# Gate, up and K with weights still: 16 wide and 16 narrow products for two weight units instead of 4 and 4 for each k

## The chip, the core and the metric

The kernel runs on one core of a Trainium2 chip. The core has a matrix engine (TensorE, in the profile PE for the products and PEld for the loads of the stationary operand), VectorE (DVE), ScalarE (ACT), GpSimd (POOL) and a queue engine SyncE (SP) that issues transfers from HBM. The engines run on their own and meet at semaphores. The metric is the device time of one execution in microseconds (us): the median of three runs of the kernel before is 992.02 us.

## The reference

A trunk of two layers over 256 tokens with 1024 channels, in float32. Each layer has a SwiGLU FFN (2816 hidden channels), a token mixer and a second such FFN, with norms around them. The mixer of layer 0 is a recurrent block (RG-LRU), that of layer 1 an attention whose K, V and forget gates are computed once from the stream after layer 0. What the change touches are the gate, up and K products:

```python
def swiglu(x, w_gate, w_up, w_down):
    return (jax.nn.silu(x @ w_gate) * (x @ w_up)) @ w_down
...
hn = rms_norm(h, g)
kv = (hn @ w_kv).reshape(Bn, S, 2, N_HEADS, HEAD_DIM)
```

## The kernel before

**Split operands.** Each weight `w` is split into a high part `whi` (ScalarE, line 204: a copy with the rounding of fp32r) and a low part `wlo` (VectorE, line 205: what is left); so is the activation (`xhi`, `xlo`, side by side in `xall`). A product takes high x high, high x low and low x high.

**Weights still.** For most gate and up tiles and for K the weights are the stationary operand and the activations move. One call of `mmj` does one k, that is 128 of the 1024 input channels, for a tile of 512 output channels: four products with a 128x128 block of `whi` over 512 moving columns (`xhi` and `xlo` of all 256 tokens, line 238; I call them wide), each into a PSUM bank of its own, then four with a block of `wlo` over the 256 columns of `xhi` alone (line 240, narrow). The left and the right half of a bank are added up later (`total`, lines 511 and 512). Elsewhere (`mm3`, lines 212 to 214, in the down projections and others) the activation stands still and 512 columns of weights move; in the recurrent block (`mm3w`, lines 219 to 221) the weights stand still and 256 columns move.

**Units and tiles.** A weight unit is 128x1024 floats: two k of one tile. One transfer brings it into one of five `raw` buffers, and the split writes it into one of nine `whi` and nine `wlo` buffers. A tile takes four units (k0 = 0, 2, 4, 6). Gate tiles accumulate in banks 4 to 7, up tiles in banks 0 to 3, in turn; the two K tiles use banks 4 to 7, then 0 to 3. While a tile is at work its banks are `lent`. Behind a tile's last product stand `gate_rows`, `up_rows` or `post_k`, each beginning with `total`. The FFNs have 44, 36, 44 and 36 units of this kind and K has 8.

**Order.** TensorE runs its instructions in the order in which the program issues them; the other engines' orders are made by a scheduler. `run_ffn` calls `slot(None, i)` for each unit of the still part, clears `state["edge"]`, and goes on with the down projection. `slot` prepares the unit where that has not been done, calls its work, marks it in `done` and ticks. `still` does the two k of a unit with a tick between them. So a unit has two ticks.

**Ticks.** `tick` counts down the deferred work in `pend` and runs what is due, and it lets `prepare_next` issue the load and the split of one unit further on, if the estimated landing time has passed and the unit nine before is done. Work deferred with the flag `calm` is held back while `state["edge"]` is true. Before the change `edge` is true in the first and the last unit of a tile and false in the two between. The calm pieces are `gains_T` for the later gains (line 162), `rg_params` (line 710), `running(0)` and `running(1)` (running sums of the forget gates, lines 1065 and 1066) and `rows(0)` and `rows(1)` (line 1072, with the store of `ckT` behind it, which attention reads back). They take a free bank from `sparebank`: one of banks 0 to 3 that is neither held nor lent, otherwise 6 or 7.

**The start.** The first tile's work is interleaved by hand through `hooks`, keyed by k (1, 3 and 4): they transpose and split the activations and split the first five units.

Of the kernel before, what the change touches and what calls it, by code (L numbers as in the profile page):

```python
# [16 lines left out]
P = 128  # L17
D = 1024
S = 256
# [28 lines left out]
def trunk_kernel(ctx: ExitStack, tc: tile.TileContext, A: dict, out: bass.AP):  # L48
    nc = tc.nc
# [11 lines left out]
    def nm(s):  # L61
        uid[0] += 1
        return f"{s}_{uid[0]}"
# [33 lines left out]
    def sparebank():  # L97
        return bank("mm" if any(i not in held and i not in lent for i in range(4)) else "tr")
# [4 lines left out]
    def tensor_work(n):  # L103
        pace["t"] += n * 0.445e-3
# [5 lines left out]
    def defer(n, fn, calm=False):  # L110
        pend.append([n, fn, calm])

    def tick():
        for p in list(pend):
            p[0] -= 1
            if p[0] < 0 and not (p[2] and state["edge"]):
                pend.remove(p)
                p[1]()
        purse[0] = min(purse[0] + SHARE, SHARE)
        if state["p"] >= OPEN:  # L120
            prepare_next()
        while queue and purse[0] > 0:
            cost, _, fn = queue.pop(0)
            purse[0] -= cost
            fn()
# [98 lines left out]
    def x_moving(k):  # L224
        return xall[:, k, :, :], xhi[:, k, :]

    def mmj(bs, wh, wl, k, moving):

        both, upper = moving(k)
        o, oh = pall, pall[:, :, :S]  # L230
        if len(both.shape) == 4:
            o = o.rearrange("p n (a t b) -> p n a t b", a=2, t=2)
            oh = oh.rearrange("p n (t b) -> p n t b", t=2)
        else:
            o = o.rearrange("p n (a b) -> p n a b", a=2)
        tensor_work(3 * S * len(bs))
        for b, w in zip(bs, wh):
            nc.tensor.matmul(o[:, b], w, both, start=k == 0, stop=False)  # L238
        for b, w in zip(bs, wl):
            nc.tensor.matmul(oh[:, b], w, upper, start=False, stop=k == 7)  # L240


    def rstd_of(ss, n, f=1.0):
# [128 lines left out]
    items = []  # L372
    units = {}
    done = {}
    state = {"p": 0, "a": 0, "b": 0, "edge": False, "look": 99}
# [23 lines left out]
    def slot(t, i):  # L399
        while state["p"] <= i:  # L400
            prepare_next(True)
        items[i][1](t, units[i])
        done[i] = done.get(i, 0) + (1 if t is not None else 2)
        if done[i] == 2:
            units.pop(i)
        tick()
# [106 lines left out]

    hooks = {}

    def still(u, k0, b0, moving=x_moving):
        if k0 == 0:
            assert not set(held) & set(range(b0, b0 + 4)), held.keys()
            lent.update(range(b0, b0 + 4))
        state["edge"] = k0 in (0, 6)  # L520
        for j in range(2):
            if k0 + j in hooks:
                hooks.pop(k0 + j)()
            cut = [slice(j * 512 + b * P, j * 512 + b * P + P) for b in range(4)]
            mmj(range(b0, b0 + 4), [u.hi[:, c] for c in cut], [u.lo[:, c] for c in cut], k0 + j, moving)
            if j == 0:
                tick()
        if k0 == 6:
            lent.difference_update(range(b0, b0 + 4))
            state["edge"] = True  # L530

    def tile_items(w, c0, b0, post, moving=x_moving):
        for k0 in range(0, 8, 2):
            def prep(k0=k0):
                return split(load_raw(w[k0 * P:(k0 + 2) * P, c0:c0 + 512].rearrange("(k p) n -> p k n", p=P), P, 1024),
                             P, 1024)

            def work(t, u, k0=k0):
                still(u, k0, b0, moving)
                if k0 == 6:  # L540
                    post(b0, 4)
            items.append((prep, work))

    def ffn_items(pool_of, wg, wu, wd, post_g, next_dests, last=False, normed=False, lead=1):
        hid = {}
        sil = {}
        box = {}

        def hid_tiles():
            if not hid:  # L550
                v = hid["all"] = pool_of().tile([P, 2, 2, 22, P], F32R, tag="hid", name=nm("hid"), bufs=1)
                hid["hhi"], hid["hlo"] = v[:, 0], v[:, 1]
            return hid["hhi"], hid["hlo"]

        def gate_tile(n):
            return pool_of().tile([P, 1024], F32, tag="sil", name=nm("sil"), bufs=1)[:, :n]

        def prod_tile(n):
            return pool_of().tile([P, 16 * HA], F32, tag="prod", name=nm("prod"), bufs=1)[:, :n]

        def post_gate(t, ps):
            if t == 0:
                box["s"] = gate_tile(1024)
            s = sil[t] = box["s"][:, t * 512:(t + 1) * 512]
            nc.scalar.activation(s, ps, AF.Silu, scale=rs[t][:, 0:1])

        def post_up(c0):
            def f(t, ps):
                if t == 0:
                    box["p"] = prod_tile(1024)  # L570
                pr = box["p"][:, t * 512:(t + 1) * 512]
                nc.vector.tensor_tensor(pr, ps, sil[t], ALU.mult)
                defer(HT, lambda: hidden_T(pr, t))

            def hidden_T(pr, t):
                hh, hl = hid_tiles()
                tp = sparebank()
                for j in range(4):
                    nc.tensor.transpose(tp[:, j * P:(j + 1) * P], pr[:, j * P:(j + 1) * P], ident)
                k0 = c0 // P  # L580
                hv = hh[:, t, k0:k0 + 4, :].rearrange("p a b -> p (a b)")
                lv = hl[:, t, k0:k0 + 4, :].rearrange("p a b -> p (a b)")
                nc.scalar.activation(hv, tp, AF.Copy)
                nc.vector.tensor_tensor(lv, tp, hv.bitcast(F32), ALU.subtract)
            return f

        def gate_rows(b, m):
            s = sil["j"] = gate_tile(m * S)
            v = s.rearrange("p (a b) -> p a b", a=m)
            total(v, b, m)  # L590
            nc.vector.tensor_tensor(v, v, rcp["v"].unsqueeze(1).to_broadcast([P, m, S]), ALU.mult)  # L591
            nc.scalar.activation(s, s, AF.Silu)  # L592

        def up_rows(b, m, k0):
            pr = prod_tile(m * S)
            hh, hl = hid_tiles()
            total(pr.rearrange("p (a b) -> p a b", a=m), b, m)
            nc.vector.tensor_tensor(pr, pr, sil["j"], ALU.mult)  # L598
            pv = pr.rearrange("p (a t b) -> p a t b", a=m, t=2)
            hv = hh[:, :, k0:k0 + m, :].rearrange("p t a b -> p a t b")  # L600
            lv = hl[:, :, k0:k0 + m, :].rearrange("p t a b -> p a t b")
            nc.scalar.activation(hv, pv, AF.Copy)  # L602
            nc.vector.tensor_tensor(lv, pv, hv.bitcast(F32), ALU.subtract)

        def last_items(c0):
            for k0 in range(0, 8, 2):
                def prep(k0=k0):
                    raw = new_raw()
                    v = raw.rearrange("p (k s n) -> p k s n", k=2, s=2)
                    for s, w in enumerate((wg, wu)):  # L610
                        nc.sync.dma_start(v[:, :, s, :], w[k0 * P:(k0 + 2) * P, c0:c0 + 256].rearrange("(k p) n -> p k n", p=P))
                    return split(raw, P, 1024)

                def work(t, u, k0=k0):
                    still(u, k0, 4)
                    if k0 == 6:
                        gate_rows(4, 2)
                        up_rows(6, 2, c0 // P)
                items.append((prep, work))

        i0 = len(items)
        for i in range(5):
            if i < lead:
                proj_items(wg, i * 512, 512, main_x, post_gate)
                proj_items(wu, i * 512, 512, main_x, post_up(i * 512))
            else:
                tile_items(wg, i * 512, 4, gate_rows)
                tile_items(wu, i * 512, 0, lambda b, m, i=i: up_rows(b, m, 4 * i))
        last_items(2560)

        def load_gb():
            box["gb"] = gain_bcast(post_g)

        ahead(i0 + 24, load_gb)

        def post_down(t, accs):
            enter(t, next_dests(t, hid), accs, box["gb"], True, last, normed)

        i2 = len(items)
        row_items(wd, [P] * 22, lambda t, k: (hid["hhi"][:, t, k, :], hid["hlo"][:, t, k, :]), post_down, 4 if last else 2)  # L640
        return i0 + 8 * lead, i2, len(items)
# [472 lines left out]
    for n in range(2):  # L1114
        tile_items(A["w_kv"], n * 512, 4 - 4 * n, post_k(n), z_moving)
# [151 lines left out]
    for i in range(OPEN):  # L1267
        u = units[i] = Unit()
# [165 lines left out]
```

## Time and profile before

| what | value |
|---|---|
| median of three runs | 992.02 us (991.96 to 992.54) |
| the profiled execution, its own time | 992.25 us |
| its span, first to last instruction | 990.5 us |
| VectorE / ScalarE busy | 68% / 57% of the span |
| mean granted TensorE clock | 0.999 |
| read from HBM | 180.09 MB, 183 GB/s over the span |

The profile is one execution. Its times are counted from the span's start. In the timeline a row gives the start, the duration (merged over instructions of one kind that follow each other, with their number behind x), the engine, the line, the operation, the output and the inputs by name, the shapes, and in brackets idle time before it with what ended it. Products on PE are pipelined, their ends are modelled and they overlap: the distance between starts tells the rate, not the duration.

### The profile page before, as it was taken

What the parts mean: (1) busy time and instruction counts of PE and PEld (TensorE: products, weight loads), DVE (VectorE), ACT (ScalarE), POOL (GpSimd) and SP (SyncE); (2) the same over time, 40 slices, a digit from 0 to 9 for tenths busy, and PEclk for the clock granted to TensorE, in tenths of its full rate; (3) what the DMA queues carried; (4) which work ended last, traced back from release to release, by engine and by line L of the source; (5) the groups of instructions that cost most, each with busy time, mean ns of one, the idle gap of its engine ahead of it and who ended that gap; (6) DMA issues with size and microseconds to landing.
All of it is one profiled execution on the core that took longest, in us unless ns stands there. A gap on an engine that the chain in (4) does not pass through costs nothing.

```text
span 990.5 us, 13894 instructions
## 1 busy us (share of the span) xinstructions
PE 979.7 (99%) x5294; PEld 835.9 (84%) x5294; DVE 675.5 (68%) x791; ACT 563.3 (57%) x740; POOL 50.9 (5%) x97
## 2 busy tenths in 40 slices
PE   9999999999999999999999999999999999999997
PEld 7888888899978888888898888888887688888885
DVE  6877664668997776664696676674488867667542
ACT  6666543559986555543565555553467665555431
POOL 3300000100003000000000000000030000000000
PEclk9999999999999999999999999999999999999999
DMA  8777646565337766545468666654585157665431
GB/s 276 259 265 232 197 151 191 166 181 158 109 105 229 235 190 186 195 151 179 116 219 277 191 179 192 193 187 162 172 291 177 42 172 238 193 192 188 159 115 42
DMA packets 94088, 182.06 MB, mean 184 GB/s; under 512 B 11822, under 2 KB 33414, under 8 KB 93894
## 3 DMA queue, kind: packets, MB, share of 16 engines
q1 hardware_dynamic: 93350, 181.10, 58.3%
q8 instruction: 41, 0.67, 0.3%
q0 software_dynamic: 640, 0.07, 0.1%
q14 instruction: 25, 0.20, 0.1%
q10 hardware_dynamic: 32, 0.01, 0.0%
HBM read 180.09 MB, written 1.06 MB: 183 GB/s over the span
## 4 chain that ended last, share of the span: by engine, by line
PE 71%; issue 21%; ACT 3%; DVE 3%; POOL 1%; DMA 1%; SPq 0%; DVEq 0%; POOLq 0%; ACTq 0%
PE pall L238 24%; PE pall L240 12%; PE pall L212 9%; PE pall L214 9%; PE pall L213 9%; PE pall L856 1%; PE pall L219 1%; PE pall L220 1%; PE pall L221 1%; DVE wlo L205 1%; DMA raw<-in_ffn_w_gate_dram 1%; PE pall L1160 1%; POOL rstd L248 1%; ACT junk L253 1%; PE pall L1187 1%
## 5 line engine op out<-in xcount | busy, mean ns | idle before, releaser
L205 DVE TENSOR_TENSOR wlo<-raw,whi 128x1024 fp32r<-128x1024 f32 (+4 forms) x328 | 392.9, 1205 | 236.4 <-ACT whi L204 235.8
L204 ACT ACTIVATE whi<-raw 128x1024 fp32r<-128x1024 f32 (+4 forms) x328 | 340.1, 1044 | 284.2 <-PE pall L214 112.7
L238 PE MATMUL pall<-xall,whi 128*128 128x512 f32 x1280 | 348.7, 394 | 0.2 <-DVE xall L1284 0.2
L238 PEld LDWEIGHTS pall<-xall,whi 128*128 128x128 f32 x1280 | 219.0, 188 | 28.8 <-DVE xall L1284 0.7
L240 PEld LDWEIGHTS pall<-xall,wlo 128*128 128x128 f32 x1280 | 195.9, 188 | 28.0
L240 PE MATMUL pall<-xall,wlo 128*128 128x256 f32 x1280 | 203.7, 281 | 0.0
L212 PE MATMUL pall<-whi,hid 128*128 128x512 f32 (+2 forms) x400 | 153.0, 382 | 0.0
L214 PE MATMUL pall<-whi,hid 128*128 128x512 f32 (+2 forms) x400 | 152.5, 381 | 0.3 <-DVE hid L276 0.3
L213 PE MATMUL pall<-wlo,hid 128*128 128x512 f32 (+2 forms) x400 | 152.4, 381 | 0.0
L214 PEld LDWEIGHTS pall<-whi,hid 128*128 128x128 f32 x400 | 75.1, 188 | 14.4 <-DVE hid L276 0.6
L212 PEld LDWEIGHTS pall<-whi,hid 128*128 128x128 f32 x400 | 75.1, 188 | 13.6
L213 PEld LDWEIGHTS pall<-wlo,hid 128*128 128x128 f32 x400 | 75.1, 188 | 13.6
L246 POOL TENSOR_SCALAR nv<-ss 128x1 f32<-128x1 f32 x24 | 10.5, 438 | 925.5 <-ACT junk L253 925.4
L212 PE MATMUL pall<-whi,xall 128*128 128x512 f32 (+2 forms) x144 | 57.3, 398 | 0.0
L214 PE MATMUL pall<-whi,xall 128*128 128x512 f32 (+2 forms) x144 | 55.2, 384 | 0.0
L213 PE MATMUL pall<-wlo,xall 128*128 128x512 f32 (+2 forms) x144 | 55.0, 382 | 0.0
L592 ACT ACTIVATE sil<-sil 128x1024 f32<-128x1024 f32 (+1 forms) x22 | 21.7, 984 | 25.3 <-DVE sil L591 25.3
L602 ACT ACTIVATE hid<-prod 128x1024 fp32r<-128x1024 f32 (+1 forms) x22 | 21.6, 984 | 20.0 <-DVE prod L598 20.0
L214 PEld LDWEIGHTS pall<-whi,xall 128*128 128x128 f32 x144 | 27.0, 188 | 5.4 <-DVE xall L276 0.3
L212 PEld LDWEIGHTS pall<-whi,xall 128*128 128x128 f32 x144 | 27.1, 188 | 4.9
L213 PEld LDWEIGHTS pall<-wlo,xall 128*128 128x128 f32 x144 | 27.1, 189 | 4.5
L316 DVE SCALAR_TENSOR_TENSOR t<-pall,rstd,gb 128x512 f32<-128x512 f32 x16 | 11.8, 747 | 26.7 <-ACT junk L253 26.7
(193 smaller groups left out, 982.0 us busy)
## 6 DMA issues: line engine op xcount, KB each, us to landing
raw<-in_ffn_w_down_dram SPq DMA_DIRECT2D x88, 512.0 KB
raw<-in_ffn_w_up_dram SPq DMA_DIRECT2D x80, 512.0 KB
raw<-in_ffn_w_gate_dram SPq DMA_DIRECT2D x78, 512.0 KB
raw<-in_rg_w_in_dram SPq DMA_DIRECT2D x20, 504.0 KB
raw<-in_ffn_w_gate_dram SPq DMA_DIRECT2D x20, 256.0 KB
raw<-in_rg_w_out_dram SPq DMA_DIRECT2D x10, 504.0 KB
raw<-in_ffn_w_up_dram SPq DMA_DIRECT2D x16, 256.0 KB
raw<-in_w_kv_dram SPq DMA_DIRECT2D x8, 512.0 KB
```

The source lines that it names most:

```text
L204: nc.scalar.activation(hi[:parts, c:c + m], rawv[:, c:c + m], AF.Copy)
L205: nc.vector.tensor_tensor(lo[:parts, c:c + m], rawv[:, c:c + m], hi[:parts, c:c + m].bitcast(F32), ALU.subtract)
L212: nc.tensor.matmul(ps, xh, wh, start=first, stop=False)
L213: nc.tensor.matmul(ps, xh, wl, start=False, stop=False)
L214: nc.tensor.matmul(ps, xl, wh, start=False, stop=last)
L219: nc.tensor.matmul(ps, wh, xh, start=first, stop=False)
L238: nc.tensor.matmul(o[:, b], w, both, start=k == 0, stop=False)
L240: nc.tensor.matmul(oh[:, b], w, upper, start=False, stop=k == 7)
L246: nc.gpsimd.tensor_scalar(v, ss[:, 0:1], ss[:, 1:2] if n == 2 else 0.0, D * EPS * f * f, ALU.add, ALU.add)
L316: nc.vector.scalar_tensor_tensor(t1[n], pf[n], r_in, gb[:, n * 512:(n + 1) * 512], ALU.mult, ALU.mult)
L592: nc.scalar.activation(s, s, AF.Silu)
L602: nc.scalar.activation(hv, pv, AF.Copy)
```

## The change

`mmj` takes a list of k instead of one k, and does the wide products of all of them before the narrow ones. `still` takes a list of units. `grouped` puts the first unit of a pair by (k0 = 0 or 4, if no hooks are left); `slot` then ticks and returns without marking it done. With the second unit the pair is done at once: 16 wide products, 16 narrow ones, then three ticks, what stands behind the tile (`post`), and the tick of `slot`. `edge` is true where the group holds the first or the last k of a tile, so in both pairs of each tile. While hooks are left, units are done one at a time and one k at a time.

```diff
-    def mmj(bs, wh, wl, k, moving):
+    def mmj(bs, parts, ks, moving):
...
+        for k, (wh, wl) in zip(ks, parts):
+            tensor_work(2 * S * len(bs))
+            for b, w in zip(bs, wh):
+                nc.tensor.matmul(o[:, b], w, moving(k)[0], start=k == 0, stop=False)
+        for k, (wh, wl) in zip(ks, parts):
+            tensor_work(S * len(bs))
+            for b, w in zip(bs, wl):
+                nc.tensor.matmul(oh[:, b], w, moving(k)[1], start=False, stop=k == 7)
...
     def slot(t, i):
         while state["p"] <= i:
             prepare_next(True)
-        items[i][1](t, units[i])
+        if items[i][1](t, units[i]):
+            tick()
+            return
...
-    def still(u, k0, b0, moving=x_moving):
+    def still(us, k0, b0, moving=x_moving):
         if k0 == 0:
             assert not set(held) & set(range(b0, b0 + 4)), held.keys()
             lent.update(range(b0, b0 + 4))
-        state["edge"] = k0 in (0, 6)
-        for j in range(2):
+        n = 2 * len(us)
+        state["edge"] = k0 == 0 or k0 + n == 8
+        parts = []
+        for u in us:
+            for j in range(2):
+                cut = [slice(j * 512 + b * P, j * 512 + b * P + P) for b in range(4)]
+                parts.append(([u.hi[:, c] for c in cut], [u.lo[:, c] for c in cut]))
+        run_ = 1 if hooks else n
+        for j in range(0, n, run_):
             if k0 + j in hooks:
                 hooks.pop(k0 + j)()
...
+            mmj(range(b0, b0 + 4), parts[j:j + run_], range(k0 + j, k0 + j + run_), moving)
+            for _ in range(run_ if j + run_ < n else run_ - 1):
                 tick()
-        if k0 == 6:
+        if k0 + n == 8:
             lent.difference_update(range(b0, b0 + 4))
             state["edge"] = True
...
+    def grouped(k0, kept, fn):
+
+        i = len(items)
+
+        def work(t, u):
+            kept.append((i, u))
+            if len(kept) < 2 and not hooks and k0 % 4 == 0:
+                return [i]
+            us = [v for _, v in kept]
+            done_ = [j for j, _ in kept]
+            del kept[:]
+            fn(us, k0 + 2 - 2 * len(us))
+            for j in done_[:-1]:
+                done[j] = 2
+                units.pop(j)
+        return work
```

`tile_items` and `last_items` build their work through `grouped`; what they load and what stands behind a tile is as before.

More of the change, by code (lines that the diff above doesn't have):

```diff
@@ L225, in x_moving @@
         return xall[:, k, :, :], xhi[:, k, :]
-    def mmj(bs, wh, wl, k, moving):
-        both, upper = moving(k)
+    def mmj(bs, parts, ks, moving):
         o, oh = pall, pall[:, :, :S]
-        if len(both.shape) == 4:
+        if len(moving(ks[0])[0].shape) == 4:
             o = o.rearrange("p n (a t b) -> p n a t b", a=2, t=2)
@@ L235, in mmj @@
             o = o.rearrange("p n (a b) -> p n a b", a=2)
[L236 to L240, printed above, removed]
+        for k, (wh, wl) in zip(ks, parts):
[6 more added lines that the diff above has]
+                nc.tensor.matmul(oh[:, b], w, moving(k)[1], start=False, stop=k == 7)
     def rstd_of(ss, n, f=1.0):
@@ L519, in still @@
             lent.update(range(b0, b0 + 4))
-        state["edge"] = k0 in (0, 6)
-        for j in range(2):
+        n = 2 * len(us)
[7 more added lines that the diff above has]
+        for j in range(0, n, run_):
             if k0 + j in hooks:
                 hooks.pop(k0 + j)()
-            cut = [slice(j * 512 + b * P, j * 512 + b * P + P) for b in range(4)]
-            mmj(range(b0, b0 + 4), [u.hi[:, c] for c in cut], [u.lo[:, c] for c in cut], k0 + j, moving)
-            if j == 0:
+            mmj(range(b0, b0 + 4), parts[j:j + run_], range(k0 + j, k0 + j + run_), moving)
+            for _ in range(run_ if j + run_ < n else run_ - 1):
                 tick()
-        if k0 == 6:
+        if k0 + n == 8:
             lent.difference_update(range(b0, b0 + 4))
             state["edge"] = True
+    def grouped(k0, kept, fn):
[12 more added lines that the diff above has]
+        return work
     def tile_items(w, c0, b0, post, moving=x_moving):
+        kept = []
         for k0 in range(0, 8, 2):
@@ L536, in prep, with go @@
                              P, 1024)
-            def work(t, u, k0=k0):
-                still(u, k0, b0, moving)
+            def go(us, k, k0=k0):
+                still(us, k, b0, moving)
                 if k0 == 6:
                     post(b0, 4)
-            items.append((prep, work))
+            items.append((prep, grouped(k0, kept, go)))
     def ffn_items(pool_of, wg, wu, wd, post_g, next_dests, last=False, normed=False, lead=1):
@@ L605, in last_items @@
         def last_items(c0):
+            kept = []
             for k0 in range(0, 8, 2):
@@ L612, in prep, with go @@
                     return split(raw, P, 1024)
-                def work(t, u, k0=k0):
-                    still(u, k0, 4)
+                def go(us, k, k0=k0):
+                    still(us, k, 4)
                     if k0 == 6:
@@ L618, in work @@
                         up_rows(6, 2, c0 // P)
-                items.append((prep, work))
+                items.append((prep, grouped(k0, kept, go)))
         i0 = len(items)
```

## The prediction

> **What bounds the kernel now.** I read the page first: the span, the busy row of TensorE (PE), the chain of waits and the costliest groups; the last row comes from the view of groups with shapes kept apart.
>
> ```profile
> span 990.5 us, 13894 instructions
> ...
> PE 979.7 (99%) x5294; PEld 835.9 (84%) x5294; DVE 675.5 (68%) x791; ACT 563.3 (57%) x740; POOL 50.9 (5%) x97
> ...
> PE 71%; issue 21%; ACT 3%; DVE 3%; POOL 1%; DMA 1%; SPq 0%; DVEq 0%; POOLq 0%; ACTq 0%
> ...
> L238 PE MATMUL pall<-xall,whi 128*128 128x512 f32 x1280 | 348.7, 394 | 0.2 <-DVE xall L1284 0.2
> ...
> L240 PE MATMUL pall<-xall,wlo 128*128 128x256 f32 x1280 | 203.7, 281 | 0.0
> ...
> L238 PE MATMUL pall<-hid,whi 128*128 128x512 f32 x64 | 17.6, 396 | 0.0
> ```
>
> PE is busy 99% and the chain runs through it. The two groups that the change reorders sat idle 0.2 us in all: they wait for nobody. So what counts is the distance from one product's start to the next (I call it the pitch; the mean of 394 ns is longer because products overlap), plus any new wait on PE. There are 1280 + 64 = 1344 wide products, eight to a weight unit: 168 units.
>
> Next I read the timeline of PE in a calm stretch of layer 0's second FFN:
>
> ```profile
> 371.30 1.09 PE L238 MATMUL pall<-xall,whi 128*128 128x512 f32 x4
> 372.23 0.64 PE L240 MATMUL pall<-xall,wlo 128*128 128x256 f32 x4
> 372.70 1.09 PE L238 MATMUL pall<-xall,whi 128*128 128x512 f32 x4
> 373.62 0.64 PE L240 MATMUL pall<-xall,wlo 128*128 128x256 f32 x4
> 374.10 1.09 PE L238 MATMUL pall<-xall,whi 128*128 128x512 f32 x4
> ...
> 427.30 1.09 PE L238 MATMUL pall<-xall,whi 128*128 128x512 f32 x4
> ```
>
> From 371.30 to 427.30 lie 40 such groups (20 units), 1.400 us each. Four wide products take 0.93 or 0.92, mean 0.925 (0.2313 each); four narrow ones 0.47 or 0.48, mean 0.475 (0.1188 each). Two units, four groups, take 5.60 us.
>
> **The change part by part.**
>
> *1. Order of the products.* Count and shapes stay; 16 wide then 16 narrow replace four times 4 and 4. Two rows of this trace show longer runs of one width. The wide one is the start of the down projection, directly behind a narrow group:
>
> ```profile
> 432.90 0.39 PE L212 MATMUL pall<-whi,hid 128*128 128x512 f32 x1
> 433.13 0.39 PE L213 MATMUL pall<-wlo,hid 128*128 128x512 f32 x1
> 433.36 0.40 PE L214 MATMUL pall<-whi,hid 128*128 128x512 f32 x1
> 433.60 0.39 PE L212 MATMUL pall<-whi,hid 128*128 128x512 f32 x1
> 433.82 0.40 PE L213 MATMUL pall<-wlo,hid 128*128 128x512 f32 x1
> 434.06 0.39 PE L214 MATMUL pall<-whi,hid 128*128 128x512 f32 x1
> 434.29 0.39 PE L212 MATMUL pall<-whi,hid 128*128 128x512 f32 x1
> ...
> 439.95 0.39 PE L213 MATMUL pall<-wlo,hid 128*128 128x512 f32 x1
> ```
>
> The first six pitches take 434.29 - 432.90 = 1.39 us (0.232 each, as in the groups of four); the next 25 take 5.66, 0.2264 each. A wide run settles after about six products; a group of four never gets there. Sixteen would cost 1.39 + 10 x 0.2264 = 3.65 us against 16 x 0.2313 = 3.70: 0.046 gained. Bounds: nothing (no settling, 0.2313), and 16 x (0.2313 - 0.2264) = 0.078 (settled from the first).
>
> The narrow run is in the recurrent block, 48 in a row with loads of 126 columns, the count from the table of stretches:
>
> ```profile
> 208.76 0.28 PE L219 MATMUL pall<-xall,whi 128*126 128x256 f32 x1
> ...
> 214.29 0.28 PE L221 MATMUL pall<-xall,wlo 128*126 128x256 f32 x1
> 208.76:214.28 5.52, 5.52 (x48) 1.00 0.58 145
> ```
>
> 47 pitches in 5.53 us: 0.1177 each, with a weight load before each as here. Sixteen cost 1.883 against 1.90: 0.017 gained. Bounds: 0.017, and a loss of 0.02 if all stand at the worst quarter of the groups above (0.48 / 4 = 0.12, so 1.92). I take the long run, the nearest in length. A pair of units gains 0.063 us.
>
> How many pairs: 84, less the first two. While the start's hooks stand, units 0 to 2 run alone, one k at a time as before, and unit 3 runs alone with two k. So 82 x 0.063 = **5.2 us gained**; by the bounds from 82 x (0 - 0.02) = 1.6 lost to 82 x 0.095 = 7.8 gained.
>
> By the Trainium skill ("TensorE: Matmul & The Clock Gate", section "Back-to-back issue gap") an isolated product's spacing follows its width alone, N/2.4 + 2.5 ns, or 215.8 and 109.2 ns for our widths, an estimate from the page. By that rule the order is worth nothing, and this part of the sum would be 0. The rows above differ with it: one width stands at 0.232 and at 0.2264 in one run.
>
> *2. Weight supply.* A pair starts when its first unit used to; it needs the second unit's high part after 8 wide products (1.85 us) instead of 2.80, the low parts later than before. It holds nine-deep buffers longer. Leads:
>
> ```profile
> 19.05 1.05 ACT L204 ACTIVATE whi<-raw 128x1024 fp32r<-128x1024 f32 x1
> 20.14 1.23 DVE L205 TENSOR_TENSOR wlo<-raw,whi 128x1024 fp32r<-128x1024 f32 x1 [1.09 <-ACT whi L204]
> 22.76 1.09 PE L238 MATMUL pall<-xall,whi 128*128 128x512 f32 x4
> 399.07 1.06 ACT L204 ACTIVATE whi<-raw 128x1024 fp32r<-128x1024 f32 x1 [1.74 <-PE pall L238]
> ```
>
> The tightest is unit 5, the first split by line 204 (the first five units are split elsewhere): high part ready at 20.10, used at 22.76. Asked for 0.95 earlier, 2.66 of lead become 1.71. Its low part (21.37) is used later. In the steady stretch the split itself waits for PE to free a buffer: weights stand as far ahead as nine buffers allow, some seven units. Giving up two of them for 5.5 us leaves five. I cost this at 0; without the cover the price is one late split, 1.05 to 1.23 us, a pair.
>
> *3. Ticks and deferred work.* A pair ticks five times instead of four, one of these right after its first unit is put by, three after all 32 products. `edge` is true in both halves of a tile, so work deferred as calm no longer runs inside one. Three pieces, `gains_T` (its product of line 162), `rg_params` (710) and `rows(1)` (1072, and behind it on SP's queue the store of `ckT`), move to the first tick of the down projection, where `edge` is false. What such an interruption costs:
>
> ```profile
> 36.79 1.09 PE L238 MATMUL pall<-xall,whi 128*128 128x512 f32 x4
> ...
> 39.99 1.08 PE L238 MATMUL pall<-xall,whi 128*128 128x512 f32 x4
> 132.70:194.00 61.30, 60.97 (x274) 50.33 (x273) 32.36 (x34) 27.41 (x35) 2.15 (x4) 1.00 0.52 164
> ```
>
> Around the product of `gains_T` two groups take 3.20 instead of 2.80: 0.40. Moved, it is paid again. VectorE (32.36 of 61.30 us busy) and ScalarE (27.41) have room for their parts in the down projection; the readers come later, and the down projection of layer 1 lasts tens of us, so SP's store is not late for attention. Net 0, bounds -1.2 to +1.2 (three of them saved or doubled).
>
> *4. A new wait.* The fourth calm piece is `running(1)`, which ran inside K:
>
> ```profile
> 518.66 1.09 PE L238 MATMUL pall<-hid,whi 128*128 128x512 f32 x4
> 525.68 0.29 PE L1065 MATMUL pall<-lf,ones 128*128 128x16 f32 x2
> 541.64 1.08 PE L238 MATMUL pall<-xall,whi 128*128 128x512 f32 x4
> 541.36 1.06 ACT L204 ACTIVATE whi<-raw 128x1024 fp32r<-128x1024 f32 x1 [1.74 <-PE pall L238]
> 542.33 1.01 ACT L511 ACTIVATE kk<-pall 128x1024 f32<-128x1024 f32 x1
> 543.60 1.22 DVE L512 TENSOR_TENSOR kk<-pall,kk 128x1024 f32<-128x1024 f32 x1
> ```
>
> It stands five groups of 1.40 behind K's start, at K's fifth tick; `edge` had been false at the third and fourth, so it was not due before. Now K's first tick alone has `edge` false, too early. The next tick with `edge` false follows the put-by first unit of layer 1's first gate tile: `run_ffn` has cleared `edge`, and no `still` has set it again. There `sparebank` gives one of banks 0 to 3, which K's second tile has just filled and `post_k` (lines 511, 512) still reads. PE must wait until line 512 ends, 543.60 + 1.22 = 544.82, while it was free for the next product at 541.64: 3.18 us. Behind it in PE's order stand all products of the gate tile. In the changed kernel the split of 541.36 comes earlier, its buffer being freed 1 us sooner, and line 511 can start some 0.5 sooner: 2.65. Upper bound: a split of 1.23 by line 205 in front of line 512, 4.4. I take **2.9 us lost**, once; its four small products were paid before.
>
> **Sum**: -5.2 + 0 + 0 + 2.9 = -2.3 us. The profiled execution took 990.5 us of span and 992.25 in all, so 989.95; it lies 0.23 over the runs' median of 992.02, hence **989.7**. Its own range takes 1.0 about the sum for the settling and 0.4 for the wait: 988.3 to 991.1.
>
> **The rivals.**
> - *No settling*: with four weight tiles and four banks in turn the wide run stays at 0.2313, narrow at 0.1188. For it: no run of more than four exists in this form. Against: the first four pitches of the down projection equal those of a group. Gain 0, wait 2.9: 994.9, **slower**. It decides from a wide pitch of 0.229 upwards: the wait takes 2.9 / 82 = 0.035 a pair, or 0.0022 for each of 16. The page's rule named above leads here too.
> - *Narrow run at 0.12*: a pair gains 0.046 - 0.02 = 0.026, 2.1 in all; +0.8: 992.8. For it: the quarters of 0.48. Against: 48 in a row at 0.1177.
> - *The wait does not come*: `running(1)` falls due in another tick, or gets a free bank. Then -5.2: 986.8. Against: the order of the code; for it, that I count ticks from one position in the trace.
> - *Slowest rows throughout*: wide 0.93 / 4 = 0.2325 (+0.02 a pair), narrow 0.12 (+0.02): 82 x 0.04 = 3.3, with the wait 998.2.
>
> **Chances.** Forecast 0.50, no settling 0.15, narrow at 0.12 0.13, no wait 0.13, slowest rows 0.09. A measurement tells 0.2% (2.0 us) from no change. The forecast's centre lies just beyond: two thirds of it (0.33) are faster, a third (0.17) the same. Faster 0.33 + 0.13 = 0.46; same 0.17 + 0.13 = 0.30; slower 0.15 + 0.09 = 0.24. The range 986.4 to 995.2 holds all but the slowest rows and some tails.
>
> **What would show it.** Right: 16 wide products that start at 0.23 and settle near 0.2266, a pair near 5.54 us, and before the first gate tile of layer 1 a gap on PE of 2.6 to 3.2 us ended by line 512 on VectorE, with lines 1065 and 1066 behind it. Wrong in step 1: pairs at 5.60; in step 2: idle time of the wide products put down to lines 204 or 205; in step 3: the down projections longer by over 1 us; in step 4: lines 1065 and 1066 elsewhere, without a gap.

## The result and the profile after

The changed kernel takes 994.95 us (median of 7 runs, 993.65 to 996.77) against 992.31 (7 runs, 991.77 to 992.56): the ratio is 1.0027, 95% interval 1.0017 to 1.0038. It is slower by 2.6 us; 989.7 had been forecast, within a range up to 995.2.

The page of the changed kernel, the lines that answer to those of before (lines 238 and 242 are the wide and the narrow products now):

```profile
span 993.2 us, 13885 instructions
...
PE 978.4 (99%) x5294; PEld 837.7 (84%) x5294; DVE 673.0 (68%) x791; ACT 566.4 (57%) x739; POOL 51.1 (5%) x97
...
PE 72%; issue 21%; DVE 3%; ACT 3%; POOL 1%; DVEq 0%; POOLq 0%; ACTq 0%
...
L238 PE MATMUL pall<-xall,whi 128*128 128x512 f32 x1280 | 308.5, 393 | 1.4 <-ACT rrow L303 0.9
...
L242 PE MATMUL pall<-xall,wlo 128*128 128x256 f32 x1280 | 166.9, 283 | 0.0
```

The busy sums fall by far more than any time gained, since overlapping products that follow each other are counted once (sixteen wide ones in a row count 3.82 us below, four counted 1.09). The useful figure is the idle column: the wide products sat idle 0.2 us before and 1.4 now. The view of PE's waits, longest first (who waited, for whom, total, times, longest), names the new ones:

```profile
PE pall L1094 <- DVE kk L516: 2.7, 1, 2.7
PE pall L156 <- DVE idle L144: 1.5, 1, 1.5
PE pall L1216 <- DVE pe L1209: 1.0, 2, 0.7
PE pall L238 <- ACT rrow L303: 0.9, 1, 0.9
```

The second and third are old. The first is the forecast one: `running(1)` (line 1094 now) waits for line 516, 512 before. The fourth had not been forecast.

The steady stretch on PE's timeline:

```profile
371.25 3.82 PE L238 MATMUL pall<-xall,whi 128*128 128x512 f32 x16
374.90 2.08 PE L242 MATMUL pall<-xall,wlo 128*128 128x256 f32 x16
376.81 3.82 PE L238 MATMUL pall<-xall,whi 128*128 128x512 f32 x16
380.47 2.08 PE L242 MATMUL pall<-xall,wlo 128*128 128x256 f32 x16
382.38 0.86 PE L238 MATMUL pall<-xall,whi 128*128 128x512 f32 x3
```

A pair takes 5.565 us (from 371.25 to 382.38 are two), against 5.60. Sixteen wide products take 3.655, as forecast from the settled run of the down projection. Sixteen narrow ones take 1.91, 0.1195 each in the mean of all such runs of the trace, not 0.1177: they cost a little more than in groups of four (0.1188).

The place of the long wait, again on PE's timeline, and the table of stretches around it (engines' busy times, then the granted clock):

```profile
534.96 3.82 PE L238 MATMUL pall<-hid,whi 128*128 128x512 f32 x16
538.61 2.07 PE L242 MATMUL pall<-hid,wlo 128*128 128x256 f32 x16
543.37 0.39 PE L1094 MATMUL pall<-lf,ones 128*128 128x16 f32 x2 [2.69 <-DVE kk L516]
543.62 0.37 PE L1095 MATMUL pall<-lf,triu 128*128 128x16 f32 x2
543.84 5.49 PE L238 MATMUL pall<-xall,whi 128*128 128x512 f32 x16
549.17 2.08 PE L242 MATMUL pall<-xall,wlo 128*128 128x256 f32 x16
...
543.80:547.30 3.50, 3.50 (x11) 2.78 (x11) 0.86 (x2) 0.00 (x0) 0.00 (x0) 0.57 0.56 200
```

PE would have been free at 538.61 + 1.91 = 540.52 and begins the gate tile at 543.84: 3.32 us. Of these, 0.44 had been paid inside K by the kernel before, where the two groups around `running(1)` take 3.24 instead of 2.80, which leaves 2.9:

```profile
524.27 1.09 PE L238 MATMUL pall<-hid,whi 128*128 128x512 f32 x4
...
527.51 1.09 PE L238 MATMUL pall<-hid,whi 128*128 128x512 f32 x4
```

And the first 16 wide products of that tile take 549.17 - 543.84 = 5.33 us instead of 3.65, while the granted clock is 0.57 in the mean of the first 3.5 us: another 1.7 us that no wait shows, since PE counts as busy.

### The profile page after: what moved, and what is told of

Read it like the earlier page. It is cut to its first block, busy times and chain, and to the rows that moved or that the text cites. A ratio compares the mean times of both kernels' runs of the same rounds, so it can differ in the third digit from the quotient of the medians.

```text
span 993.2 us, 13885 instructions
## 1 busy us (share of the span) xinstructions
PE 978.4 (99%) x5294; PEld 837.7 (84%) x5294; DVE 673.0 (68%) x791; ACT 566.4 (57%) x739; POOL 51.1 (5%) x97
## 4 chain that ended last, share of the span: by engine, by line
PE 72%; issue 21%; DVE 3%; ACT 3%; POOL 1%; DVEq 0%; POOLq 0%; ACTq 0%
PE pall L238 24%; PE pall L242 13%; PE pall L212 9%; PE pall L214 9%; PE pall L213 9%; PE pall L885 1%; DVE wlo L205 1%; PE pall L219 1%; PE pall L220 1%; PE pall L221 1%; PE pall L1189 1%; ACT whi L204 1%; PE pall L1216 1%; POOL rstd L250 1%; ACT junk L255 0%
## 5 line engine op out<-in xcount | busy, mean ns | idle before, releaser
L205 DVE TENSOR_TENSOR wlo<-raw,whi 128x1024 fp32r<-128x1024 f32 (+4 forms) x328 | 388.3, 1205 | 245.7 <-ACT whi L204 109.8
L238 PE MATMUL pall<-xall,whi 128*128 128x512 f32 x1280 | 308.5, 393 | 1.4 <-ACT rrow L303 0.9
L238 PEld LDWEIGHTS pall<-xall,whi 128*128 128x128 f32 x1280 | 236.1, 189 | 47.8 <-ACT rrow L303 1.1
L242 PEld LDWEIGHTS pall<-xall,wlo 128*128 128x128 f32 x1280 | 164.7, 191 | 6.9 <-DVE wlo L1321 0.4
L242 PE MATMUL pall<-xall,wlo 128*128 128x256 f32 x1280 | 166.9, 283 | 0.0
L515 ACT ACTIVATE sil<-pall 128x1024 f32<-128x1024 f32 (+1 forms) x22 | 20.9, 949 | 19.6 <-PE pall L242 19.6
L515 ACT ACTIVATE prod<-pall 128x1024 f32<-128x1024 f32 (+1 forms) x22 | 20.9, 949 | 18.0 <-PE pall L242 18.0
```

The lines of the kernel that those rows point to most:

```text
L205: nc.vector.tensor_tensor(lo[:parts, c:c + m], rawv[:, c:c + m], hi[:parts, c:c + m].bitcast(F32), ALU.subtract)
L238: nc.tensor.matmul(o[:, b], w, moving(k)[0], start=k == 0, stop=False)
L242: nc.tensor.matmul(oh[:, b], w, moving(k)[1], start=False, stop=k == 7)
L515: nc.scalar.activation(v, pall[:, b:b + m, S:], AF.Copy)
```

## The experiments

My theory after this reading had four terms: 82 pairs gain 0.035 each (-2.9 us); the wait costs 2.9; the clock that falls after it 1.7; the first pair's wait on line 303 0.9. They sum to +2.6. Times below are medians; a ratio is against the kernel before, measured beside it.

| run | what it is | us | ratio (95%) |
|---|---|---|---|
| e1_edge | changed, `edge` kept true | 990.41 | 0.9984 (0.9975 to 0.9992) |
| e2_filled | changed, the idle time filled with work | 995.65 | 1.0034 (1.0022 to 1.0047) |
| e3_first | changed, unit 3 by single k | 994.04 | 1.0018 (1.0009 to 1.0027) |
| e4_both | e1 and e3 | 989.68 | 0.9974 (0.9964 to 0.9985) |
| e5_eight | e4, 8 and 8 | 990.77 | 0.9987 (0.9978 to 0.9995) |
| e6_tile | e4, 32 and 32 | 992.28 | 1.0002 (0.9993 to 1.0011) |
| e7_bank | e4, narrow products bank by bank | 989.64 | 0.9975 (0.9965 to 0.9984) |
| e8_short | e4, narrow products of 192 columns | 977.98 | 0.9857 (0.9843 to 0.9870) |
| e9_load128 | e4, loads of 128 columns in the recurrent block | 988.94, one run | |
| e10_tile_late | e6 without the ticks of put-by units | 994.01 | 1.0016 (1.0006 to 1.0025) |
| e11_tile_mixed | e6, pairs where `hidden_T` is due | 988.43 | 0.9963 (0.9949 to 0.9977) |
| e12_shifted | e4, narrow blocks begin every 126 columns | 987.87, one run | |

**e1_edge: take the wait away.**

```diff
         if items[i][1](t, units[i]):
+            state["edge"] = True
             tick()
```

> The tick after a put-by first unit now has edge true, so running(1) waits for layer 1's down projection instead of running before its first gate tile. Theory: the wait of 2.7 us on line 516 goes, and with it the 3.4 us of half clock behind it, which cost another 1.65; the small products are paid later. 994.95 - 2.85 - 1.65 = about 990.5 us, no row of half clock, mean clock 0.999. Rival (the slow wide products of that gate tile come from something else than the idle time, its weights or its banks): they stay at 0.43 us each, and only the wait goes: 992.1.

990.41 was measured, 4.54 under the changed kernel. PE's timeline over the same place has no gap, and the gate tile's wide products take 3.65:

```profile
539.13 2.08 PE L242 MATMUL pall<-hid,wlo 128*128 128x256 f32 x16
541.04 3.82 PE L238 MATMUL pall<-xall,whi 128*128 128x512 f32 x16
544.69 2.08 PE L242 MATMUL pall<-xall,wlo 128*128 128x256 f32 x16
```

The slow products went with the wait, so the rival that put them down to their weights or banks falls. `running(1)`, now in the down projection, costs there what it had cost inside K: from the product before it to the second behind it 0.91 us go by, where two pitches would take 0.46, so 0.45.

```profile
664.67 0.40 PE L214 MATMUL pall<-whi,hid 128*128 128x512 f32 x1
664.90 0.29 PE L1095 MATMUL pall<-lf,ones 128*128 128x16 f32 x2
...
665.58 0.39 PE L213 MATMUL pall<-wlo,hid 128*128 128x512 f32 x1
```

**e2_filled: leave the wait's place, take the idleness away.**

```diff
         if t == 1:
+            ps = trbank()
+            for _ in range(24):
+                nc.tensor.matmul(ps[:, :P], kv["ones"], kv["triu"], start=True, stop=True)
```

> 24 small products into a bank that nobody reads stand in front of running(1), some 2.6 us of work in the place of the idle time. Nothing else is changed, so line 1094's place and the wait for line 516 stay. Theory (idle time brings the clock down): the products of the gate tile behind it start at 0.23 us each, 16 of them in 3.75 instead of 5.33; 994.95 - 1.65 = about 993.3 us, mean clock 0.999. Rival (weights or banks): 16 wide products still take 5.3 us, 994.9. If the wait alone decides and the extra products come on top of it: 997.

The time, 995.65, missed all three figures. PE's timeline and the stretch behind the gap say why:

```profile
540.50 5.52 PE L1096 MATMUL pall<-triu,ones 128*128 128x128 f32 x48
545.86 0.29 PE L1097 MATMUL pall<-lf,ones 128*128 128x16 f32 x2
546.00 0.37 PE L1098 MATMUL pall<-lf,triu 128*128 128x16 f32 x2
546.22 3.91 PE L238 MATMUL pall<-xall,whi 128*128 128x512 f32 x16
549.98 2.08 PE L242 MATMUL pall<-xall,wlo 128*128 128x256 f32 x16
...
543.80:547.30 3.50, 3.50 (x29) 3.33 (x29) 0.93 (x2) 0.00 (x0) 0.00 (x0) 1.00 0.51 183
```

Each of my 24 float32 products became two instructions (x48), 5.36 us of work in place of 2.85, so the gate tile began 2.4 us later than in the changed kernel. But its 16 wide products took 549.98 - 546.22 = 3.76 at a clock of 1.00 (3.75 had been expected), instead of 5.33 at 0.57. So 994.95 + 2.4 - 1.6 = 995.75, and 995.65 was measured. The place and the order of the products are those of the changed kernel, only the idle time is filled, and all five runs have a mean clock of 0.999: what halves the clock is the idle time. How much it costs changes from run to run: the fastest run of the changed kernel, 993.65, has a mean clock of 0.999, the middle ones 0.997, and the slowest, 996.77, 0.994. The Trainium skill's page "TensorE: Matmul & The Clock Gate", section "Part 1: The HAM clock gate", has the clock halved after at least one idle window of about 3.4 us, and the window is free-running, so that the start of a kernel does not reset it. The trace agrees that the halved clock follows idle time, but not in the length: 2.7 us of waiting were enough in most runs. That the loss changes from run to run would fit a window that starts anywhere; no run here shows the window itself.

**e3_first: the wait at the start.** In the first tile `rstd_rows` had run between the two k of unit 3. With both k done at once it came after them, and its result sits in one of banks 0 to 3, which the next tile needs at once; line 303 reads that bank behind the `total` of the tile just done. ScalarE in the changed kernel:

```profile
19.40 1.02 ACT L515 ACTIVATE sil<-pall 128x1024 f32<-128x1024 f32 x1 [1.44 <-PE pall L242]
20.32 0.38 ACT L303 ACTIVATE rrow<-pall 128x256 f32<-128x256 f32 x1
```

The edit lets the first tile go by single k:

```diff
+    first = [1]
...
-        run_ = 1 if hooks else n
+        run_ = 1 if hooks or first else n
...
             state["edge"] = True
+            first.clear()
```

> Unit 3 goes one k at a time again, so rstd_rows comes between its two k as before the change. Theory: line 303 reads its bank before the next tile needs it, the wait of 0.9 us of the first pair on it goes, and the tile starts at 20.0 instead of 20.75: 994.95 - 0.8 = about 994.1 us. Rival (the time is only moved: the first pair then waits for the splits): first pair unchanged at 20.7, 994.9.

994.04: 0.91 less (among the runs with a mean clock of 0.997 alone, 995.0 and 994.0), with the second tile beginning at 19.89 instead of 20.75:

```profile
19.89 2.44 PE L238 MATMUL pall<-xall,whi 128*128 128x512 f32 x10
```

**e4_both: the order of the products alone.**

> Both edits together; what is left of the change is the order of the products. Theory: 82 pairs at 5.566 instead of 5.601 us, 2.9 us gained on 992.3, calm work moved at no cost: about 989.6 us. Rival (the pairs' gain is given back in other places): 992 or more.

989.68: 5.27 under the changed kernel, where e1 and e3 together promise 5.45, and 2.6 under the kernel before, where 82 pairs promise 2.9. The four terms stand to within 0.3 us, and the idea of the change was right: its order of products is worth 0.26%.

**e5_eight, e6_tile, e10_tile_late and e11_tile_mixed: how long a run?** Only the condition under which `grouped` puts a unit by differs, and for e10 the tick:

```diff
-            if len(kept) < 2 and not hooks and k0 % 4 == 0:
+            if False:                                                                       # e5
+            if not hooks and k0 < 6:                                                        # e6, e10
+            if not hooks and k0 < 6 and len(kept) < (4 if all(p[2] for p in pend) else 2):  # e11
```

> With the two edits of e4, but units go alone: 8 wide products, 8 narrow, a tick after both. Theory (a wide run settles after six products, so two of eight gain): a unit 1.841 + 0.951 = 2.792 us as unit 3 in the changed kernel, against 2.801 before: 165 x 0.009 = 1.4 us, about 990.9 us. Rival (the gain comes from pairing, buffers and ticks and not from the length of the run): 992.3.

> With the two edits of e4, and four units together: 32 wide products, then 32 narrow ones, a whole tile. Theory: 1.388 + 26 x 0.2267 + 32 x 0.1195 = 11.106 us a tile against 2 x 5.567 = 11.134 in pairs: 41 x 0.028 = 1.1 us, so 988.5 us. Rival (four of nine buffers in use leave too few ahead): wide products wait for lines 204 or 205 and it is slower than 989.7.

> As e6, 32 wide and 32 narrow products, but no tick when a unit is put by. Theory: e6 lost its gain since the ticks of put-by units bring the four transposes of hidden_T forward, and PE waits 1.66 us for their input twice, 3.3 us; now they come inside the first tile's end and no wait is left: 989.7 - 1.1 = about 988.6 us. Rival (the loss of e6 lies in the long group itself, its buffers or its load order): 991 or more.

> As e6, but while a deferred piece that is not calm stands in the list (hidden_T, at the start of the FFNs with a moving first tile), units go in pairs; all other tiles are whole, 32 and 32. Theory (e6 and e10 lost at hidden_T alone, too early and too late): no wait on lines 603 or 613, 38 or 39 whole tiles gain 0.02 to 0.03 us each on e4: 988.6 to 988.9 us. Rival (whole tiles cost elsewhere): 989.7 or more.

PE's timeline of e5 and, below, of e6 in the same tile:

```profile
599.73 2.00 PE L238 MATMUL pall<-xall,whi 128*128 128x512 f32 x8
601.57 1.12 PE L242 MATMUL pall<-xall,wlo 128*128 128x256 f32 x8
602.52 2.00 PE L238 MATMUL pall<-xall,whi 128*128 128x512 f32 x8
```

```profile
596.41 7.44 PE L238 MATMUL pall<-xall,whi 128*128 128x512 f32 x32
603.69 4.00 PE L242 MATMUL pall<-xall,wlo 128*128 128x256 f32 x32
607.52 4.72 PE L238 MATMUL pall<-xall,whi 128*128 128x512 f32 x20
...
PE pall L610 <- DVE prod L603: 3.3, 2, 1.7
```

Eight wide products take 1.84 and eight narrow 0.95, so a unit takes 2.79 instead of 2.80, and e5's 990.77 lies 1.4 under its kernel before, as worked out. In e6 a narrow product still takes 3.83 / 32 = 0.1197, and a tile takes 607.52 - 596.41 = 11.11, as worked out. Yet e6 missed: 992.28 came instead of 988.5. Most of that is lost where a first tile follows a moving one. There the ticks of put-by units bring the transposes of `hidden_T` forward, and PE waits for their input twice (the last row, from the view of waits). Without those ticks they come too late, and the next tile waits for their bank:

```profile
PE pall L238 <- DVE hid L613: 3.2, 2, 1.8
```

e10 missed too, with 994.01 instead of 988.6: I had seen one side of that boundary. The waits bring e6 to 991.8 and e10 to 991.8; the 0.5 that e6 took beyond it, and the 0.9 of e10's profiled run (992.65), stay open. The median of e10 holds more than its waits: four of its eleven runs took 992.6 to 992.9 at a mean clock of 0.998 or 0.999, the other seven 993.8 to 994.4 at 0.997. That is a loss of the size and kind of the changed kernel's, though the two waits in the trace, 490 us apart, are only 1.4 and 1.8 us long. The trace is of one of the four, so which wait brings the clock down in the others, and how long it is there, is not shown. e11 goes in pairs while `hidden_T` is outstanding, has neither wait, and with 988.43, a little under the 988.6 to 988.9 worked out, beats both kernels, by 3.8 and 6.5 us, and e4 by 1.2.

**e7_bank, e8_short, e9_load128 and e12_shifted: why a narrow product takes 0.1195 here and 0.1177 in the recurrent block.** The comments name the run; in e8's 96, the 192 columns lie in two parts.

```diff
+        for j, b in enumerate(bs):                                                      # e7
+            for k, (wh, wl) in zip(ks, parts):
+                nc.tensor.matmul(oh[:, b], wl[j], moving(k)[1], start=False, stop=k == 7)
...
+                m = moving(k)[1]                                                        # e8
+                q = 192 if len(m.shape) == 2 else 96
+                nc.tensor.matmul(oh[:, b, :q] if len(m.shape) == 2 else oh[:, b, :, :q], w, m[:, :q] if len(m.shape) == 2 else m[:, :, :q], start=False, stop=k == 7)
...
+                        m = P if w == RT and j == 0 else w                              # e9
...
+                low = [slice(j * 512 + b * 126, j * 512 + b * 126 + P) for b in range(4)]  # e12
```

> With the two edits of e4, the 16 narrow products in the order of banks: four k for one bank, then the next, as the products of the recurrent block stay in one bank. Theory (the narrow pitch of 0.1195 is set by the load of 128 columns ahead of each product, 126 in the recurrent block): 0.1195 as before, 989.7 us. Rival (it is the change of bank with each product): 0.1177, and 82 x 16 x 0.0018 = 2.4 us less, 987.3.

> With the two edits of e4, the narrow products take 192 of the 256 moving columns; the low part of the weights is left out for the other 64 tokens. Theory (the load of 128 columns sets the narrow pitch): it stays near 0.1195 and the time near 989.7 us. Rival (the moving columns set it): it falls by 64 / 2400 = 0.027 to 0.093 and the time by 82 x 16 x 0.027 = 35 us, to 955.

> With the two edits of e4. In the recurrent block the first 24 of each 48 products load 128 weight columns instead of 126 (the two more give two rows that nobody reads), the second 24 load 126 as before. Theory (the columns of the load make the difference between 0.1195 and 0.1177): the first 24 pitches at 0.1195, the second at 0.1177. Rival (it is something else in the still tiles, such as their operands or banks): both at 0.1177. The time, 989.7 us, tells neither.

> With the two edits of e4; the narrow products' blocks of 128 weight columns begin every 126 columns, as in the recurrent block, instead of every 128, so that the low parts belong to other channels than they should. Theory (where the block begins in its row makes the difference between 0.1195 and 0.1177): the narrow pitch falls to 0.1177 or under, 82 x 16 x 0.0018 = 2.4 us less than 989.7. Rival: it stays at 0.1195 and the cause is still open.

Narrow runs on PE's timelines, each with the row that follows it, of e7, e8, e9 (first and last of the 24 with 128 columns, first with 126, and the product behind the run) and e12:

```profile
604.69 2.08 PE L243 MATMUL pall<-xall,wlo 128*128 128x256 f32 x16
606.60 3.82 PE L238 MATMUL pall<-xall,whi 128*128 128x512 f32 x16
```

```profile
607.31 1.93 PE L244 MATMUL pall<-xall,wlo 128*128 128x192 f32 x16
609.08 3.15 PE L238 MATMUL pall<-xall,whi 128*128 128x512 f32 x13
```

```profile
207.72 0.28 PE L219 MATMUL pall<-xall,whi 128*128 128x256 f32 x1
...
210.40 0.28 PE L221 MATMUL pall<-xall,wlo 128*128 128x256 f32 x1
210.51 0.28 PE L219 MATMUL pall<-xall,whi 128*126 128x256 f32 x1
...
213.32 0.39 PE L212 MATMUL pall<-whi,xall 128*128 128x504 f32 x1
```

```profile
608.98 2.06 PE L242 MATMUL pall<-xall,wlo 128*128 128x256 f32 x16
610.87 1.32 PE L238 MATMUL pall<-xall,whi 128*128 128x512 f32 x5
```

e7: 1.91 / 16, unchanged, so the bank is not it. e8: 1.77 / 16 = 0.1106, with a quarter of the columns left out. If the columns alone set the pitch it would be near 0.093, an estimate from the wide and the narrow pitch: 0.1195 - 64 x (0.2267 - 0.1195) / 256. If the load alone, 0.1195. So neither expectation holds: the pitch falls by a third of what the columns would give, and something beside them counts. A floor near 0.11 that the load of 128 weight columns sets would fit, but a single width does not show it. The Trainium skill's page "TensorE: Matmul & The Clock Gate", section "LDWEIGHTS (loading the stationary operand)", gives columns / 1.2 ns for a load; for 128 columns that is an estimate of 107 ns, near e8's pitch. The trace can't confirm it: the median row of a load lasts 192 ns in e8, and the loads begin 0.11 us apart, so their rows overlap and don't tell the rate. e9: 24 pitches in 2.79 with loads of 128 columns, 24 in 2.81 with 126, 0.116 and 0.117. So 128 columns against 126 in a load are not what makes the difference, and my theory of it falls. e12: 1.89 / 16 = 0.118 (0.1183 in the mean of all such runs of the trace). Two thirds of the difference go with the position at which a block begins in its row, and the time falls with it: 82 x 16 x 0.0012 = 1.6 us, 989.68 to 987.87 in the one run. (A single run tells this roughly: e9's lay 0.7 under e4's median too.) What makes the rest, and why the position matters, stays open. (e12's low parts belong to other channels; it is a measurement and no version.)

## Why the prediction was wrong

*Wide products (step 1).* Right: 3.65 per pair had been read from the start of the down projection, 3.655 came.

*Narrow products (step 1).* Mis-sized. I took 0.1177 from the recurrent block as "the long run, the nearest in length"; 0.1195 came, the rival "narrow run at 0.12". A pair gains 0.035 instead of 0.063 us, 82 of them 2.9 instead of 5.2: 2.3 us of the miss. The nearest row in form, the groups of four with the same operands, had said 0.1188, nearer but still too low; e12 shows that where the weight blocks begin in their rows is a part of the form. What makes the rest stays open.

*Weight supply (step 2).* Right: no PE wait on lines 204 or 205 in the changed kernel.

*Ticks and deferred work (step 3).* "Net 0" held within 0.3 us for the pieces named, as e4 shows, which moves all four. But the list was short: `rstd_rows` is deferred too, and in the first tile it moved from between unit 3's two k to behind them. What I had looked for were calm pieces; this one isn't. 0.9 us (e3).

*The new wait (step 4).* Place, cause and size were right: 2.69 idle, 2.9 net, line 1094 released by line 516 on VectorE and line 1095 right behind it. What failed was to stop there: "2.9 us lost, once" counts the gap and not what a gap of that length does to the clock. Another 1.7 us (e1 and e2).

So the forecast of -2.3 misses 2.3 + 0.9 + 1.7 = 4.9 us, which gives +2.6, as measured. The rival "no settling" named nearly the measured time, 994.9, and was wrong in its mechanism: the wide runs settle. That its number agrees is luck.

## What to carry to other kernels

Price a run of products by a row of the same form first and the same length second; the operands' place can be worth as much as the order. Where a change regroups instructions, go through every deferred piece and ask between which products it now falls, and which buffer or bank its neighbours need. An idle gap on the matrix engine can cost more than its length, as the 2.7 us here did in most runs and, by its mean clocks, perhaps e10's waits of under 2 us in some: look at the granted clock behind it, since the slow products show up as busy time.

## What the runs showed of the hardware

- A run of 512-column products settles from about 0.231 us to 0.2267 after about six: with weights still, eight take 1.84, sixteen 3.655 and 32 take 7.28 (603.69 - 596.41 in e6); with activations still, six pitches took 0.232 and the next 25 took 0.2264. It starts anew after every narrow run.
- 2.7 us of waiting brought the granted clock to 0.57 over the next 3.5 us in the profiled run, at a cost of 1.7; the same place kept busy stayed at 1.00 (e2).
- Sixteen narrow products take 1.91 us with weight blocks that begin every 128 columns and 1.89 with blocks that begin every 126.
- With 192 instead of 256 moving columns a narrow product falls from 0.1195 to 0.1106 only.
